# The in-projection of a short convolution by seven half-size products instead of eight, and weights laid out in order of use

## The chip, the cores and the metric

One NeuronCore of a Trainium2 chip runs the whole program in one launch. The metric is the device time of one execution in microseconds. Times of the kernel before: three runs, median 1492.78 us (1491.48 to 1495.35). TensorE (PE) does the matrix products, VectorE (DVE) and ScalarE (ACT) the elementwise work, GpSimd (POOL) a little, and SyncE (SP) issues the loads. A matmul multiplies a stationary block of 128x128 weights with up to 512 columns of tokens and adds into PSUM.

## The reference

Four layers, each with its own token mixer (HGRN2, short convolution, RG-LRU, latent attention), over 512 latent and 128 prompt tokens, T = 640 in all, at width 1024:

```
x <- LayerNorm(alpha * x + gate * Mixer(x * (1 + scale) + shift))
```

Scale, shift and gate come from a conditioning vector times a 1024x3072 matrix per layer (`ada_w`). The change is in layer 1, whose mixer is, for the modulated input h:

```
bg, cg, v, g = split(h @ w_in, 4)          # w_in is 1024 x 4096
y = depthwise_conv(cg * v, width 3) + b
out = (bg * y * silu(g)) @ w_out
```

## The kernel before, in words

All products are float32 by three products of a rounded form: each operand is kept as a high part (`xh`, `wh`) and a low part (`xl`, `wl`), and hi x hi, hi x lo and lo x hi are added in PSUM. Tokens lie along the free dimension, as 8 blocks (KT = 8) of 128 channels by 640 tokens.

Weights come in blocks of 128 x 1024 numbers (512 KB). `_prep` (L57) loads one into a raw tile (L71, for a column block of 128 outputs in runs of 128 numbers, 512 B), has ScalarE cast the high part (L74) and VectorE subtract it for the low part (L76, at high priority). Raw tiles have 3 buffers (NR, tag `wraw`), high and low tiles 4 (NW). `next_w` (L94) keeps three blocks ready ahead, and before that pumps the ada units: each call adds a rate (0.4 in this stage) to a credit, and a whole credit runs one `ada_unit` (L205), two loads of 512 KB into the same raw tiles and 8 matmuls (L230) of the conditioning of a later layer, summed by VectorE at L232.

`sconv` (L806) runs over j = 0..7, and for each takes four output tiles of 128 channels, in the order cg, v, bg, g. A tile is made by `mtile` (L120): 8 blocks x 3 products x 2 token halves = 48 matmuls of 320 columns (L136) into two PSUM banks. ScalarE copies cg (L821), VectorE multiplies it with v straight from PSUM (L823), ScalarE makes the middle tap (L828), VectorE the two outer ones in four pieces (L803), multiplies by bg (L840), and applies silu(g) (ScalarE tanh at L386, L388) into `o` (L843), the input of the out-projection (`pso`, L116 to L118). For j = 0 the first pair, and for j = 7 the last, run by `mpair` (L140), which takes two tiles together in token pieces of 384 and 256, since the next or the last tokens come late. Between, `affine` (L292, L293) finishes tokens of the layer before.

PSUM has two buffers of two banks for these tiles (`psmm`) and four of one bank for all else (`psg`). A list scheduler with priorities sets the order of the instructions of each engine; each engine then runs its own in that order, and waits on tiles as a whole: an instruction that overwrites a tile waits for its readers.

Of the kernel before, what the change touches and what calls it, by code (L numbers as in the profile page):

```python
# [16 lines left out]
P = 128  # L17
# [28 lines left out]

class Kernel:
# [4 lines left out]
    def weights(self, items):  # L52
        self.wq = list(items)
        self.wready = []
        self.wpos = 0

    def _prep(self):  # L57
        nc = self.nc
        parts = self.wq[self.wpos]
        if isinstance(parts, tuple):  # L60
            parts = [parts]
        i = self.wpos
        self.wpos += 1
        n = sum(a * b for _, (a, b) in parts)
# [12 lines left out]
        self.wready.append(res)  # L77
# [42 lines left out]
    def mtile(self, nk=KT, xh=None, xl=None, halves=False):  # L120
# [17 lines left out]
        return out  # L138

# [65 lines left out]
    def ada_unit(self, l, c, u):  # L205
# [15 lines left out]
        for k in (2 * u, 2 * u + 1):  # L221
            raw = self.rawp.tile([P, 1024], F32, name=f"araw{l}_{c}_{k}", tag="wraw")
            w = self.I["ada_w"][l][k * P:(k + 1) * P, :]
            if c == 2:
                nc.sync.dma_start(out=raw, in_=w[:, 2 * D:3 * D])
            else:
                nc.sync.dma_start(out=raw.rearrange("p (a n) -> p a n", a=2),
                                  in_=w.rearrange("p (a n) -> p a n", a=3)[:, 0:2, c * 512:(c + 1) * 512])
# [115 lines left out]
    def norm_tile(self, l, i, s, stats, tp, last):  # L344
# [19 lines left out]
        def rest():  # L364
            for j0 in range(0, KT, 4):
                h = tp.tile([P, 4, P], F32, name="hm", tag="hm")
# [34 lines left out]
    def start(self):  # L401

        nc, tc = self.nc, self.tc
        with ExitStack() as ctx:
# [29 lines left out]
            def part(q, u):  # L434

                raw = tp.tile([P, 2, 2, 256], F32, name=f"araw0_{q}_{u}", tag="araw", bufs=NA)
                for k in range(2):
                    w = self.I["ada_w"][0][(2 * u + k) * P:(2 * u + k + 1) * P, :].rearrange("p (a n) -> p a n", a=3)
                    nc.sync.dma_start(out=raw[:, k], in_=w[:, 0:2, q * 256:(q + 1) * 256])
# [36 lines left out]

    def hgrn_weights(self):
        w = self.I["hg_w_in"]
        it = []

        def col(c0):
            return (w[:, c0:c0 + P].rearrange("(k p) n -> p k n", p=P), (KT, P))
        for kind, h in self.HG_ORDER:
            if kind == "g":
                it.append(col(4096 + h * P))
                continue
            it.append(col(1024 + h * P))
            it.append(col(2048 + h * P))
            it.append(col(h * P))
            if h % 2 == 0:  # L490
                for kk in range(2):
                    it.append((w[kk * 512:(kk + 1) * 512, 3072 + h * P:3072 + (h + 2) * P]
                               .rearrange("(k p) n -> p k n", p=P), (4, 256)))
        return it + self.out_weights(self.I["hg_w_out"])

    @staticmethod
    def out_weights(w):
        it = []
        for c0 in (0, 256):
            for kk in range(2):  # L500
                it.append((w[kk * 512:(kk + 1) * 512, c0:c0 + 256].rearrange("(k p) n -> p k n", p=P), (4, 256)))
        for kk in range(4):
            it.append((w[kk * 256:(kk + 1) * 256, 512:1024].rearrange("(k p) n -> p k n", p=P), (2, 512)))
        return it
# [283 lines left out]
    def sconv_weights(self):  # L788
        w = self.I["sc_w_in"]
        it = []  # L790
        for j in range(KT):
            for g in (1, 2, 0, 3):
                c0 = g * D + j * P
                it.append((w[:, c0:c0 + P].rearrange("(k p) n -> p k n", p=P), (KT, P)))
        return it + self.out_weights(self.I["sc_w_out"])

# [9 lines left out]
    def sconv(self):  # L806
        nc, tc = self.nc, self.tc
        with ExitStack() as ctx:
            sp = ctx.enter_context(tc.tile_pool(name="sp", bufs=1))
            for j in range(KT):  # L810
                cg = sp.tile([P, T], F32, name="cg", tag="cg")
                p = sp.tile([P, T], F32, name="pcv", tag="pcv")
                if j == 0:
                    pss = self.mpair()
                    for hf in range(2):
                        c = SPL[hf]
                        nc.scalar.copy(out=cg[:, c], in_=pss[hf][:, 0])
                        nc.vector.tensor_tensor(out=p[:, c], in0=cg[:, c], in1=pss[hf][:, 1], op=ALU.mult)
                else:
# [10 lines left out]
                bz = sp.tile([P, T], F32, name="bz", tag="bz")  # L830
                if j == KT - 1:
                    pss = self.mpair()
                    for hf in range(2):
                        c = SPL[hf]
                        nc.vector.tensor_tensor(out=bz[:, c], in0=zz[:, c], in1=pss[hf][:, 0], op=ALU.mult)
                        sg = self.silu2h(sp, pss[hf][:, 1], ("silut", "sg")[hf])
                        nc.vector.scalar_tensor_tensor(out=self.o[:, j, c], in0=sg, scalar=0.5, in1=bz[:, c], op0=ALU.mult, op1=ALU.mult)
                    break
                ps = self.mtile()
                nc.vector.tensor_tensor(out=self.hv(bz), in0=self.hv(zz), in1=ps, op=ALU.mult)  # L840
                ps = self.mtile()
                sg = self.silu2(sp, ps, "sg")
                nc.vector.scalar_tensor_tensor(out=self.o[:, j, :], in0=sg, scalar=0.5, in1=bz, op0=ALU.mult,  # L843
                                               op1=ALU.mult)
                if 1 <= j <= NT:
                    self.affine(0, j - 1)

# [3 lines left out]

    def rg_weights(self):
        w, wg = self.I["rg_w_in"], self.I["rg_w_gate"]
        it = []
        for kind, r in self.RG_ORDER:
            if kind == "b":
                for d in range(2):
                    it.append((wg[d, r].rearrange("(k p) n -> p k n", p=P), (2, 512)))
            else:
                for a in range(2):  # L860
                    c0 = (D if kind == "g" else 0) + (2 * r + a) * P
                    it.append((w[:, c0:c0 + P].rearrange("(k p) n -> p k n", p=P), (KT, P)))
        return it + self.out_weights(self.I["rg_w_out"])
# [152 lines left out]

    def mla_weights(self):
        w, wq, wkv = self.I["mla_w_in"], self.I["mla_w_qb"], self.I["mla_w_kvb"]

        def blk(m, r0, nr, c0, nco):  # L1020
            return (m[r0 * P:(r0 + nr) * P, c0:c0 + nco].rearrange("(k p) n -> p k n", p=P), (nr, nco))
        gt = [blk(w, 0, KT, 672 + j * P, P) for j in range(KT)]
        it = gt[:2] + [blk(w, 2 * i, 2, 0, 384) for i in range(4)]
        it += [blk(w, 3 * i, min(3, KT - 3 * i), 384, 288) for i in range(3)] + gt[2:]
        it += [blk(wq, 0, 2, 1024, 512), blk(wq, 2, 1, 1024, 512)]
        for g in range(4):
            it.append(blk(wkv, 0, 2, 1024 + g * 256, 256))
            for p in range(2):
                c = (2 * g + p) * P
                it.append([blk(wkv, 0, 2, c, P), blk(wq, 0, 3, c, P)])  # L1030
        return it + self.out_weights(self.I["mla_w_out"])
# [388 lines left out]
    def build(self):  # L1420
# [50 lines left out]

def _consts():
# [57 lines left out]
```

## Time and profile before

| | |
|---|---|
| median of three runs | 1492.78 us |
| the profiled execution | 1496.1 us, span 1494.2 us |
| TensorE, matmuls | 1443.9 us busy, 97% of the span, 10738 records |
| VectorE | 998.2 us, 67% |
| ScalarE | 695.6 us, 47% |
| GpSimd | 91.8 us, 6% |
| chain that ended last, by engine | PE 72%, DVE 13%, ACT 8%, DMA 3% |
| L136 of that chain | 26% |
| loads by the SP queue | 153.58 MB, 32.8% of 16 engines' span |

A busy time is the union of an engine's records. A chain is followed back from the last instruction, at each step to what released it. Matmuls overlap in their records: what one costs is the distance from start to start. The short-convolution stage lies between about 516 and 800 us, its in-projection between 516 and 757.9.

### The profile page before, as it was taken

What the parts mean: (1) busy time and instruction counts of PE and PEld (TensorE: products, weight loads), DVE (VectorE), ACT (ScalarE), POOL (GpSimd) and SP (SyncE); (2) the same over time, 40 slices, a digit from 0 to 9 for tenths busy, and PEclk for the clock granted to TensorE, in tenths of its full rate; (3) what the DMA queues carried; (4) which work ended last, traced back from release to release, by engine and by line L of the source; (5) the groups of instructions that cost most, each with busy time, mean ns of one, the idle gap of its engine ahead of it and who ended that gap; (6) DMA issues with size and microseconds to landing.
All of it is one profiled execution on the core that took longest, in us unless ns stands there. A gap on an engine that the chain in (4) does not pass through costs nothing.

```text
span 1494.2 us, 26291 instructions
## 1 busy us (share of the span) xinstructions
PE 1443.9 (97%) x10738; PEld 1322.2 (88%) x10738; DVE 998.2 (67%) x1833; ACT 695.6 (47%) x1213; POOL 91.8 (6%) x194
## 2 busy tenths in 40 slices
PE   6999999999999999999999999999999999999997
PEld 4888989989989899999997889899899988888796
DVE  4677677477576734444376799787746778677767
ACT  2556456356353522122225477733642366666630
POOL 0000000000000100000001011120110200000002
PEclk8999999999999999999999999999999999999999
DMA  9422334224326144435431344443123200001031
GB/s 322 134 65 78 93 101 147 91 67 140 103 63 239 57 130 124 141 114 156 128 113 57 113 156 145 129 152 123 53 81 99 82 19 17 25 21 37 29 141 71
DMA packets 159192, 155.25 MB, mean 104 GB/s; under 512 B 6288, under 2 KB 130272, under 8 KB 159072
## 3 DMA queue, kind: packets, MB, share of 16 engines
q1 hardware_dynamic: 159072, 153.58, 32.8%
q8 instruction: 84, 1.38, 0.4%
q14 instruction: 36, 0.29, 0.1%
HBM read 147.07 MB, written 6.48 MB: 103 GB/s over the span
## 4 chain that ended last, share of the span: by engine, by line
PE 72%; DVE 13%; ACT 8%; DMA 3%; issue 3%; POOL 1%; SPq 1%; POOLq 0%; DVEq 0%; ACTq 0%
PE psmm L136 26%; PE pso L116 4%; PE pso L118 4%; PE pso L117 4%; PE poa L1345 3%; DVE wl L76 2%; PE ptp L1332 2%; PE psmm L117 2%; PE psmm L118 2%; PE psmm L960 2%; PE psmm L116 2%; PE psA L230 2%; PE psS L116 1%; PE psS L118 1%; PE psS L117 1%
## 5 line engine op out<-in xcount | busy, mean ns | idle before, releaser
L136 PE MATMUL psmm<-xh,wh 128*128 128x320 f32 x1200 | 283.8, 316 | 2.5 <-ACT vt L604 2.1
L136 PE MATMUL psmm<-xl,wh 128*128 128x320 f32 x1200 | 277.9, 312 | 0.0
L136 PE MATMUL psmm<-xh,wl 128*128 128x320 f32 x1200 | 276.3, 311 | 0.0
L74 ACT CAST wh<-wraw 128x1024 fp32r<-128x1024 f32 (+3 forms) x157 | 156.4, 1005 | 150.9 <-PE pso L118 55.6
L76 DVE TENSOR_TENSOR wl<-wraw,wh 128x1024 fp32r<-128x1024 f32 (+3 forms) x157 | 182.3, 1170 | 57.2 <-ACT wh L74 57.0
L136 PEld LDWEIGHTS psmm<-xh,wh 128*128 128x128 f32 x1200 | 200.6, 189 | 15.9 <-issue 7.5
L136 PEld LDWEIGHTS psmm<-xl,wh 128*128 128x128 f32 x1200 | 201.6, 189 | 3.7 <-issue 3.4
L136 PEld LDWEIGHTS psmm<-xh,wl 128*128 128x128 f32 x1200 | 201.9, 189 | 0.7 <-issue 0.5
L116 PE MATMUL pso<-wh,xh 128*128 128x256 f32 (+1 forms) x464 | 149.7, 323 | 0.0
L117 PE MATMUL pso<-wl,xh 128*128 128x256 f32 (+1 forms) x464 | 148.6, 320 | 0.0
L118 PE MATMUL pso<-wh,xl 128*128 128x256 f32 (+1 forms) x464 | 148.6, 320 | 0.0
L118 PEld LDWEIGHTS pso<-wh,xl 128*128 128x128 f32 x464 | 87.3, 188 | 7.3
L116 PEld LDWEIGHTS pso<-wh,xh 128*128 128x128 f32 x464 | 87.4, 188 | 7.1 <-ACT xh L104 0.4
L117 PEld LDWEIGHTS pso<-wl,xh 128*128 128x128 f32 x464 | 87.4, 188 | 6.6
L1316 ACT ACTIVATE pe<-psS,mx 128x768 f32<-128x768 f32 (+1 forms) x80 | 63.7, 797 | 38.9 <-DVE mx L1314 38.4
L1314 DVE TENSOR_REDUCE mx<-psS 128x1 f32<-128x768 f32 (+1 forms) x80 | 65.3, 817 | 7.8 <-PE psS L118 7.1
L373 ACT ACTIVATE hm<-pt,ab 128x128 f32<-128x128 f32 x108 | 41.1, 463 | 50.0 <-PE pt L369 50.0
L117 PE MATMUL psmm<-xl,wh 128*128 128x384 f32 (+1 forms) x192 | 59.8, 311 | 1.6 <-DVE xl L107 1.6
L118 PE MATMUL psmm<-xh,wl 128*128 128x384 f32 (+1 forms) x192 | 59.2, 308 | 1.1 <-DVE wl L76 1.1
L116 PE MATMUL psmm<-xh,wh 128*128 128x384 f32 (+1 forms) x192 | 59.7, 311 | 0.0
L1332 PE MATMUL ptp<-ident,pe 128*128 128x128 f32 x400 | 56.7, 273 | 0.8 <-ACT pe L1316 0.8
L326 DVE TENSOR_TENSOR t<-pso,gateb 128x256 f32<-128x256 f32 (+1 forms) x58 | 29.4, 511 | 37.1 <-PE pso L118 35.9
(424 smaller groups left out, 3013.7 us busy)
## 6 DMA issues: line engine op xcount, KB each, us to landing
araw<-in_ada_w SPq DMA_DIRECT2D x80, 512.0 KB
wraw<-in_hg_w_in SPq DMA_DIRECT2D x40, 512.0 KB
wraw<-in_sc_w_in SPq DMA_DIRECT2D x32, 512.0 KB
araw<-in_ada_w SPq DMA_DIRECT2D x32, 256.0 KB
wraw<-in_rg_w_in SPq DMA_DIRECT2D x16, 512.0 KB
wraw<-in_hg_w_out SPq DMA_DIRECT2D x8, 512.0 KB
gateb<-gate_dram SPq DMA_DIRECT2D x8, 512.0 KB
wraw<-in_sc_w_out SPq DMA_DIRECT2D x8, 512.0 KB
```

Source lines behind the costliest of these rows:

```text
L74: self.tc.keep_in_program_order(nc.scalar.copy(out=wh[:, :n], in_=raw[:, :n]))
L76: nc.vector.tensor_tensor(out=wl[:, :n], in0=raw[:, :n], in1=wh[:, :n].bitcast(F32), op=ALU.subtract)
L116: nc.tensor.matmul(ps, lhsT=ah, rhs=bh, start=(i == 0), stop=False)
L117: nc.tensor.matmul(ps, lhsT=ah, rhs=bl, start=False, stop=False)
L118: nc.tensor.matmul(ps, lhsT=al, rhs=bh, start=False, stop=(i == n - 1))
L136: nc.tensor.matmul(ps[hf][:, :HALF], lhsT=w[:, k, :], rhs=x[:, k, hf * HALF:(hf + 1) * HALF], start=(first and k == 0), stop=(last and k = ...
L230: nc.tensor.matmul(ps[32 * j:32 * j + 32, :], lhsT=self.csil[:, k, :], rhs=raw[:, j * 256:(j + 1) * 256], start=(k == 2 * u), stop=(k == 2 ...
L373: nc.scalar.activation(out=h[:, j, :], in_=pt[:, j, :], func=AF.Identity, scale=sc, bias=bi)
L1314: nc.vector.reduce_max(out=mx, in_=ps[:, :nk], axis=AX.X, negate=True)
L1316: nc.scalar.activation(out=pe[:, :nk], in_=ps[:, :nk], func=AF.Exp, bias=mx[:, 0:1], accum_out=g["sm"][:, n, hp:hp + 1])
L1332: nc.tensor.transpose(pt[:, kk, :], pe[:, (k0 + kk) * P:(k0 + kk + 1) * P], self.ident)
L1345: nc.tensor.matmul(po[hp * 64:(hp + 1) * 64, 0, :nq], lhsT=v4[:, kt, vc + hp * 64:vc + (hp + 1) * 64], rhs=g["pt"][hp][:, kk, :nq], start= ...
```

## The change

Four things are done.

**Pairs by seven products.** Two output tiles of a pair and the two token halves make a 2x2 block product, with the 8 channel blocks in two groups of 4. `spair` computes it by Strassen's scheme with seven products a, b, s2, s1, s3, s4, d, each 4 blocks x 3 = 12 matmuls of 320 columns: 84 in place of 96. Product a runs into one half of a PSUM tile (`psxz`), is copied out (L224) and kept, and s2 and s3 go on in the same half, with a copy behind each; s1 and s4 use the other half, b a bank of its own (`psy`); d ends the first half. VectorE and ScalarE form the outputs (L234, L241, L242, L245). All pairs of the stage run so but the first of j = 0.

**Weight sums.** `_prep_pair` loads a pair's two blocks, A|B and D|C, casts and splits A|B (tile `w`), and D (tile `wd`, one buffer), adds in place in the raw tiles (L111: D' = C - or + D and so on, four adds of 512), and casts and splits the sums into `ws` (s1, s3; two buffers) and another `w` tile (s2, s4). `next_w` prepares a pair where 4 blocks have room.

**Token sums.** `token_sums` forms three sums of the token blocks from h, which layer 0's norm now leaves in `self.o`, by four VectorE operations of 4 x 320, and splits four.

**Layout.** The host packs all weight blocks into `wpack` in order of use, so that each partition's row of a block is one run of 4 KB; `ada_first` and `ada_rest` do the same for the conditioning matrix. The first ada loads are 16 of 512 KB, before 32 of 256 KB.

The core of the diff:

```diff
     def _prep(self):
...
-        for src, (a, b) in parts:
-            nc.sync.dma_start(out=raw[:, o:o + a * b].rearrange("p (a b) -> p a b", a=a), in_=src)
+        w0 = P * self.woff[i]
+        nc.sync.dma_start(out=raw[:, :n], in_=self.I["wpack"][w0:w0 + P * n].rearrange("(p n) -> p n", p=P))
+        for _, _, a, _, b in parts:
...
+    def _prep_pair(self):
...
+        (a, b), (d, c) = ((r[:, 0:512], r[:, 512:1024]) for r in raws)
+
+        def halves(pool, nm, n):
+            return [pool.tile([P, n], F32R, name=f"{nm}{s}{i}", tag=f"{nm}{s}", bufs=1 if n == 512 else None)
+                    for s in "hl"]
+
+        def cast(o, r):
+            for k in range(0, r.shape[-1], 512):
+                nc.scalar.copy(out=o[0][:, k:k + 512], in_=r[:, k:k + 512])
+
+        def low(o, r):
+            nc.vector.tensor_tensor(out=o[1], in0=r, in1=o[0].bitcast(F32), op=ALU.subtract)
+
+        def add(o, x, y):
+            nc.vector.tensor_tensor(out=o, in0=x, in1=y, op=ALU.add)
+        wab, wd, s13, s24 = (halves(self.wp, "w", 1024), halves(self.sw, "wd", 512), halves(self.sw, "ws", 1024),
+                             halves(self.wp, "w", 1024))
+        with self.tc.high_priority():
+            cast(wab, raws[0])
+            cast(wd, d)
+            low(wab, raws[0])
+            low(wd, d)
+            add(d, c, d)
+            add(c, a, c)
+            cast(s13, raws[1])
+            add(a, d, a)
+            add(b, a, b)
+            cast(s24, raws[0])
+            low(s13, raws[1])
+            low(s24, raws[0])
...
     def next_w(self):
-        self.pump(self.rate)
-        la = NW - 1
-        while len(self.wready) < la and self.wpos < len(self.wq):
-            self._prep()
-        return self.wready.pop(0)
+        self.pump(self.rate * (2 if self.wready and self.wready[0][0] == 2 else 1))
+        while self.wpos < len(self.wq):
+            have = sum(n for n, _ in self.wready)
+            if isinstance(self.wq[self.wpos], Pair):
+                if self.sw is None or have + 2 > NW:
+                    break
+                self._prep_pair()
...
+    def spair(self, pool, n):
...
+        prod(x, "a", [v[:, lo, N1] for v in (self.xh, self.xl)], True)
+        p1 = keep(x, "p1")
+        prod(y, "b", [v[:, hi, N1] for v in (self.xh, self.xl)], True)
+        prod(x, "s2", t[2], False)
+        u2 = keep(x, "u2")
+        with self.tc.high_priority():
+            nc.vector.tensor_tensor(out=oa[:, N1], in0=p1, in1=y, op=ALU.add)
+        prod(z, "s1", t[1], True)
+        p5 = keep(z, "p5")
+        prod(x, "s3", t[3], False)
+        u3 = keep(x, "u3", "p1")
+        prod(z, "s4", [v[:, hi, N2] for v in (self.xh, self.xl)], False)
+        with self.tc.high_priority():
+            nc.vector.scalar_tensor_tensor(out=ob[:, N2], in0=u3, scalar=-1.0, in1=p5, op0=ALU.mult, op1=ALU.subtract)
+            nc.vector.tensor_tensor(out=oa[:, N2], in0=u2, in1=z, op=ALU.add)
+        prod(x, "d", t[4], False)
+        with self.tc.high_priority():
+            nc.scalar.mul(out=ob[:, N1], in_=x, mul=-1.0)
+        return oa, ob
...
     def sconv(self):
...
+            self.sw = ctx.enter_context(tc.tile_pool(name="sw", bufs=2))
...
-                    ps = self.mtile()
-                    nc.scalar.copy(out=self.hv(cg), in_=ps)
-                    ps = self.mtile()
-                    nc.vector.tensor_tensor(out=self.hv(p), in0=self.hv(cg), in1=ps, op=ALU.mult)
+                    p, v = self.spair(sp, 0)
+                    nc.vector.tensor_tensor(out=p, in0=p, in1=v, op=ALU.mult)
...
+                bg, g = self.spair(sp, 1)
```

Line numbers of the changed kernel that the orders below show: L95 the load of a pair's raw tile, L105 the casts, L108 the low parts, L111 the adds, L218 the matmuls, L224 the copies, L234, L241, L242 and L245 the outputs, L890 the taps, L911 cg times v, L916 the middle tap, L921 to L925 bg, silu and `o`. `wdh60` is the high part of the d block of the pair of weight blocks 60 and 61, `wdl60` its low part, `wsh60` and `wsl60` its sums s1 and s3; `wh60` and `wl60` stand for its A|B, and under the later numbers 6488 and 6489 for its sums s2 and s4; `t2h`, `t2l` and so on are the token sums.

**TensorE, in the middle of the stage, between two tiles, before.** `wh58` and `wh59` are the weight blocks of two tiles:

```order
L136 MATMUL psmm_6415<-xh_102,wh58_6270 128x320 x2
L136 MATMUL psmm_6415<-xl_103,wh58_6270 128x320 x2
L136 MATMUL psmm_6415<-xh_102,wl58_6271 128x320 x2
L136 MATMUL psmm_6471<-xh_102,wh59_6340 128x320 x2
L136 MATMUL psmm_6471<-xl_103,wh59_6340 128x320 x2
```

**TensorE, at the third product of the pair 60, now.** Ahead of these rows stand the 12 matmuls of product d of the pair 58 and nine of product b of the pair 60:

```order
L218 MATMUL psy_6654<-xl_103,wh60_6482 128x320
L218 MATMUL psy_6654<-xh_102,wl60_6483 128x320
L218 MATMUL psxz_6653<-t2h_5851,wh60_6488 128x320
L218 MATMUL psxz_6653<-t2l_5852,wh60_6488 128x320
L218 MATMUL psxz_6801<-xh_102,wh62_6630 128x320
L218 MATMUL psxz_6801<-xl_103,wh62_6630 128x320
L218 MATMUL psxz_6653<-t2h_5851,wl60_6489 128x320
```

Where a tile's matmuls followed those of the tile before, s2 now follows b, with two matmuls of product a of the pair 62 between its own first ones.

**ScalarE at the same place, before**, with `sgt` the tanh of g, `cg` the copy and `zz` the middle tap:

```order
L74 CAST wh58_6270<-wraw58_6269 128x1024
L821 COPY cg_6267<-psmm_6275 128x640
L74 CAST wh59_6340<-wraw59_6339 128x1024
L828 ACTIVATE zz_6395<-pcv_6268,vec_72 128x640
L74 CAST wh60_6410<-wraw60_6409 128x1024
L74 CAST wh61_6466<-wraw61_6465 128x1024
L386 ACTIVATE sgt_6520<-psmm_6471 128x640
L74 CAST wh62_6544<-wraw62_6543 128x1024
```

**ScalarE, now.** `psxz_6505` belongs to the pair 58, `psxz_6653` to the pair 60:

```order
L224 COPY u3_6576<-psxz_6505 128x320
L224 COPY p1_6669<-psxz_6653 128x320
L105 CAST wdh60_6484<-wraw61_6480 128x512
L245 ACTIVATE cb1_6508<-psxz_6505 128x320
L922 ACTIVATE th_6605<-cb1_6508 128x640
L105 CAST wsh60_6486<-wraw61_6480 128x512 x2
L105 CAST wh60_6488<-wraw60_6478 128x512
L105 CAST wh62_6630<-wraw62_6626 128x512 x2
L105 CAST wh60_6488<-wraw60_6478 128x512
L224 COPY u2_6695<-psxz_6653 128x320
```

The cast of a block depended on its load and on a free tile three blocks back; now the cast of `wdh60` stands behind the copies of the pair 58 and writes the one `wd` tile, which product d of the pair 58 reads.

**VectorE at the same place, before**, with `pcv` the product cg times v:

```order
L76 TENSOR_TENSOR wl58_6271<-wraw58_6269,wh58_6270 128x1024
L292 TENSOR_TENSOR z_5047<-z_5047,lng0_6261 128x1024
L293 TENSOR_TENSOR z_5047<-z_5047,lnb0_6263 128x1024
L232 TENSOR_TENSOR arows2_5864<-psA2_0_3_6325,arows2_5864 128x256
L76 TENSOR_TENSOR wl59_6341<-wraw59_6339,wh59_6340 128x1024
L823 TENSOR_TENSOR pcv_6268<-cg_6267,psmm_6345 128x640
L254 SCALAR_TENSOR_TENSOR mods2_85<-psT2_0_6402,vec_72 128x4 x4
```

**VectorE, now**, the same pair 60:

```order
L108 TENSOR_TENSOR wdl60_6485<-wraw61_6480,wdh60_6484 128x512
L111 TENSOR_TENSOR wraw61_6480<-wraw61_6480 128x512
L234 TENSOR_TENSOR ca0_6655<-p1_6669,psy_6654 128x320
L111 TENSOR_TENSOR wraw61_6480<-wraw60_6478,wraw61_6480 128x512
L923 SCALAR_TENSOR_TENSOR cb1_6508<-th_6605,cb1_6508 128x640
L111 TENSOR_TENSOR wraw60_6478<-wraw61_6480,wraw60_6478 128x512
L108 TENSOR_TENSOR wsl60_6487<-wraw61_6480,wsh60_6486 128x1024
L111 TENSOR_TENSOR wraw60_6478<-wraw60_6478 128x512
L925 SCALAR_TENSOR_TENSOR o_104<-cb1_6508,ca1_6507 128x640
L108 TENSOR_TENSOR wl60_6489<-wraw60_6478,wh60_6488 128x1024
```

Between two low parts there stood the elementwise work of one tile; now the low part of d, four in-place adds and two more low parts stand in one run, with L234, L923 and L925 between them.

## Rows read from the trace of the kernel before

**Rows 1.** Page, section 1: busy time, share of the span, instructions of each engine.
```profile
PE 1443.9 (97%) x10738; PEld 1322.2 (88%) x10738; DVE 998.2 (67%) x1833; ACT 695.6 (47%) x1213; POOL 91.8 (6%) x194
```

**Rows 2.** Windows: span, busy PE, PEld, DVE, ACT, POOL, clock, DMA share, GB/s.
```profile
550.00:575.00 25.00, 25.00 (x180) 24.22 (x180) 8.71 (x12) 4.55 (x5) 0.00 (x0) 1.00 0.46 141
```

**Rows 3.** Chain of waits, sconv stage: start, duration, engine, tile, line, count.
```profile
533.04 14.29 PE psmm L136 x96
547.33 1.00 PE psA L230 x16
...
757.93 0.12 PE pso L116
```

**Rows 4.** Timeline of PE, 552 to 580: start, duration, instruction, count.
```profile
554.82 0.46 PE L136 MATMUL psmm<-xl,wh 128*128 128x320 f32 x2
555.11 0.46 PE L136 MATMUL psmm<-xh,wl 128*128 128x320 f32 x2
```

**Rows 5.** Groups by line and form, 520 to 750: busy, mean ns, idle before.
```profile
L76 DVE TENSOR_TENSOR wl<-wraw,wh 128x1024 fp32r<-128x1024 f32 x32 | 38.8, 1221 | 24.9 <-ACT wh L74 24.9
L803 DVE SCALAR_TENSOR_TENSOR zz<-pcv,vec,zz 128x511 f32<-128x511 f32 x16 | 12.0, 748 | 6.2 <-ACT zz L828 6.2
L843 DVE SCALAR_TENSOR_TENSOR o<-sg,bz 128x640 f32<-128x640 f32 x7 | 5.8, 822 | 0.1
L803 DVE SCALAR_TENSOR_TENSOR zz<-pcv,vec,zz 128x127 f32<-128x127 f32 x16 | 5.5, 345 | 0.0
L107 DVE TENSOR_TENSOR xl<-hm,xh 128x512 fp32r<-128x512 f32 x3 | 2.0, 691 | 0.1
L104 ACT CAST xh<-hm 128x512 fp32r<-128x512 f32 x3 | 1.9, 620 | 0.1
L817 ACT COPY cg<-psmm 128x384 f32<-128x384 f32 x1 | 0.5, 472 | 0.0
```

**Rows 6.** Timeline of DVE, 572 to 590.
```profile
580.33 1.22 DVE L76 TENSOR_TENSOR wl<-wraw,wh 128x1024 fp32r<-128x1024 f32 x1
581.46 1.22 DVE L292 TENSOR_TENSOR z<-z,lng 128x1024 f32<-128x1024 f32 x1
582.72 1.23 DVE L293 TENSOR_TENSOR z<-z,lnb 128x1024 f32<-128x1024 f32 x1
```

**Rows 7.** Timeline of ACT, 553 to 580.
```profile
555.66 0.69 ACT L821 COPY cg<-psmm 128x640 f32<-128x640 f32 x1 [6.66 <-PE psmm L136]
...
571.40 1.05 ACT L74 CAST wh<-wraw 128x1024 fp32r<-128x1024 f32 x1 [5.99 <-DMA wraw<-in_sc_w_in]
```

**Rows 8.** Timeline of SP, the queue that issues the loads, 560 to 575.
```profile
567.36 3.29 SPq L71 DMA_DIRECT2D wraw<-in_sc_w_in  x2
```

**Rows 9.** Timeline of PE around an idle stretch in HGRN2.
```profile
314.75 0.66 PE L680 MATMUL pst<-ident,ku 128*128 128x128 f32 x4 [2.07 <-DVE ku L675]
...
315.86 0.73 PE L136 MATMUL psmm<-xh,wl 128*128 128x320 f32 x2
316.39 0.73 PE L136 MATMUL psmm<-xh,wh 128*128 128x320 f32 x2
```

**Rows 10.** Windows of 1 us behind that idle stretch.
```profile
315.00:316.00 1.00, 1.00 (x8) 1.00 (x7) 0.95 (x3) 1.00 (x3) 0.00 (x0) 0.73 0.00 0
...
318.00:319.00 1.00, 1.00 (x7) 1.00 (x7) 1.00 (x4) 0.28 (x1) 0.00 (x0) 0.57 0.00 0
```

**Rows 11.** Chain of waits at the start of the program.
```profile
16.87 7.18 DMA araw<-in_ada_w
24.09 1.29 PE psQ L443 x16
```

**Rows 12.** Windows of 2 us: loads in 1-KB runs, loads in 4-KB runs.
```profile
28.00:30.00 2.00, 2.00 (x22) 0.98 (x21) 0.00 (x0) 0.00 (x0) 0.00 (x0) 0.82 1.09 384
...
1436.00:1438.00 2.00, 2.00 (x19) 2.00 (x18) 0.68 (x3) 0.00 (x0) 0.00 (x0) 1.00 1.02 410
```

More of the change, by code (lines that the diff above doesn't have):

```diff
@@ L44 @@
 NVEC = _o
+class Pair(list):
+    pass
 class Kernel:
@@ L53, in weights @@
         self.wq = list(items)
+        self.woff = [0]
+        for parts in self.wq:
+            self.woff.append(self.woff[-1] + sum(a * b for _, _, a, _, b in parts))
         self.wready = []
@@ L59, in _prep @@
         parts = self.wq[self.wpos]
-        if isinstance(parts, tuple):
-            parts = [parts]
         i = self.wpos
         self.wpos += 1
-        n = sum(a * b for _, (a, b) in parts)
+        n = sum(a * b for _, _, a, _, b in parts)
         raw = self.rawp.tile([P, 1024], F32, name=f"wraw{i}", tag="wraw")
@@ L76, in _prep, with part @@
             nc.vector.tensor_tensor(out=wl[:, :n], in0=raw[:, :n], in1=wh[:, :n].bitcast(F32), op=ALU.subtract)
-        self.wready.append(res)
+        self.wready.append((1, res))
+    def _prep_pair(self):
+        nc = self.nc
+        i = self.wpos
+        self.wpos += 2
+        raws = []
+        for n in range(2):
+            raw = self.rawp.tile([P, 1024], F32, name=f"wraw{i + n}", tag="wraw")
+            w0 = P * self.woff[i + n]
+            nc.sync.dma_start(out=raw, in_=self.I["wpack"][w0:w0 + P * 1024].rearrange("(p n) -> p n", p=P))
+            raws.append(raw)
+        (a, b), (d, c) = ((r[:, 0:512], r[:, 512:1024]) for r in raws)
[24 more added lines that the diff above has]
+            low(s24, raws[0])
+        def part(o, k):
+            return [x[:, 512 * k:512 * k + 512].rearrange("p (a b) -> p a b", a=4) for x in o]
+        self.wready.append((2, dict(a=part(wab, 0), b=part(wab, 1), d=part(wd, 0), s1=part(s13, 0), s3=part(s13, 1),
+                                    s2=part(s24, 0), s4=part(s24, 1))))
     def pump(self, rate):
@@ L138, in mtile, with prod, keep @@
         return out
+    def spair(self, pool, n):
+        nc = self.nc
+        w = self.next_w()
+        N1, N2 = slice(HALF, T), slice(0, HALF)
+        lo, hi = slice(0, 4), slice(4, KT)
+        t = self.tops
+        xz = self.psmm.tile([P, 2, 512], F32, name="psxz", tag="mm")
+        y = self.psg.tile([P, 512], F32, name="psy", tag="g")
+        x, z, y = xz[:, 0, :HALF], xz[:, 1, :HALF], y[:, :HALF]
+        def prod(ps, wk, b, first):
+            (ah, al), (bh, bl) = w[wk], b
+            for k in range(4):
+                for u, v, st, en in ((ah, bh, True, False), (ah, bl, False, False), (al, bh, False, True)):
+                    nc.tensor.matmul(ps, lhsT=u[:, k, :], rhs=v[:, k, :], start=(first and st and k == 0),
+                                     stop=(en and k == 3), skip_group_check=True)
+        def keep(ps, nm, tag=None):
+            o = pool.tile([P, HALF], F32, name=nm, tag=tag or nm)
+            with self.tc.high_priority():
+                nc.scalar.copy(out=o, in_=ps)
+            return o
+        oa = pool.tile([P, T], F32, name=f"ca{n}", tag=f"ca{n}")
+        ob = pool.tile([P, T], F32, name=f"cb{n}", tag="cb")
+        prod(x, "a", [v[:, lo, N1] for v in (self.xh, self.xl)], True)
[14 more added lines that the diff above has]
+        prod(x, "d", t[4], False)
+        with self.tc.high_priority():
+            nc.scalar.mul(out=ob[:, N1], in_=x, mul=-1.0)
+        return oa, ob
@@ new lines, in token_sums, with parts @@
+    def token_sums(self, pool):
+        nc, o = self.nc, self.o
+        N1, N2 = slice(HALF, T), slice(0, HALF)
+        lo, hi = slice(0, 4), slice(4, KT)
+        b11, b12, b21, b22 = o[:, lo, N1], o[:, lo, N2], o[:, hi, N1], o[:, hi, N2]
+        def parts(n):
+            return [pool.tile([P, 4, HALF], F32R, name=f"t{n}{s}", tag=f"t{n}{s}") for s in "hl"]
+        t = {1: [v[:, lo, N2] for v in (self.xh, self.xl)], 2: parts(2), 3: parts(3), 4: parts(4)}
+        nc.vector.tensor_tensor(out=b11, in0=b11, in1=b12, op=ALU.subtract)
+        nc.vector.tensor_tensor(out=b12, in0=b22, in1=b12, op=ALU.subtract)
+        nc.vector.scalar_tensor_tensor(out=b22, in0=b22, scalar=-1.0, in1=b11, op0=ALU.mult, op1=ALU.subtract)
+        self.split(*t[2], b22)
+        self.split(*t[1], b11)
+        self.split(*t[3], b12)
+        nc.vector.scalar_tensor_tensor(out=b21, in0=b22, scalar=-1.0, in1=b21, op0=ALU.mult, op1=ALU.subtract)
+        self.split(*t[4], b21)
+        self.tops = t
@@ L222, in ada_unit @@
             raw = self.rawp.tile([P, 1024], F32, name=f"araw{l}_{c}_{k}", tag="wraw")
[L223 to L228, printed above, removed]
+            nc.sync.dma_start(out=raw, in_=self.I["ada_rest"][l, c, k])
             for j in range(4):
@@ L436, in part @@
                 raw = tp.tile([P, 2, 2, 256], F32, name=f"araw0_{q}_{u}", tag="araw", bufs=NA)
-                for k in range(2):
-                    w = self.I["ada_w"][0][(2 * u + k) * P:(2 * u + k + 1) * P, :].rearrange("p (a n) -> p a n", a=3)
-                    nc.sync.dma_start(out=raw[:, k], in_=w[:, 0:2, q * 256:(q + 1) * 256])
+                nc.sync.dma_start(out=raw.rearrange("p k a n -> p (k a n)"), in_=self.I["ada_first"][4 * q + u])
                 ps = acc[q % 2][:, q - q % 2, :]
@@ L829, in sconv @@
                 self.taps(zz, p, (-1, 1), (cw(0), cw(2)))
[L830 to L838, printed above, removed]
```

175 lines of the change are left out of this document (91 added, 84 removed).

## The prediction

> **What bounds the kernel now.** I read the page's busy times first: TensorE is busy for 97% of the span, VectorE for 67%, ScalarE for 47% [rows 1]. An average over eleven stages does not say what this stage hides, so I read windows of 25 us over the short-convolution stage next: TensorE is busy in every microsecond at the full granted clock, VectorE for 8.7 of 25 us [rows 2]. Then the chain of waits: it runs on TensorE alone, 96 matmuls of the in-projection in 14.29 us, two ada units of 8 matmuls each in 1.00 us, and the next stage's first matmul at 757.93 [rows 3]. The pitch of two 320-column matmuls in the timeline is 0.29 us, so 0.147 us each [rows 4]; the 0.46 us beside it is the modelled record of two overlapping ones, not their price. So before, every matmul that goes is time, provided that its operands are ready. What I have to find out is whether they are.
>
> **What the change takes from TensorE.** Fifteen pairs lose 12 of 96 matmuls: 15 x 12 x 0.147 = 26.5 us. A pair took 14.29 us, and 14.7 with its ada share: 0.4 units for each of its two blocks, a unit being 8 matmuls or 0.5 us [rows 3]. It would take 84 x 0.147 + 0.4 = 12.7 us. This is the gain if nothing waits.
>
> **What it adds: a chain that can't start early.** `wd` has one buffer. The orders show what follows: ScalarE's cast of the next pair's d block can't be made until product d of the pair before has read the old one, and product d is a pair's last. Behind that cast stand, each on the one before: the low part of d, the add that overwrites d in the raw tile, the add into c, the add into a, the add into b, the cast of that sum, its low part, and only then s2, the third product. Call the end of product d zero and count a link at a time. Durations: 1.22 us for a low part of 1024, 0.82 for 640, 0.75 for a tap of 511, 0.35 for one of 127, 0.69 for 512, 0.62 for ScalarE's cast of 512, 0.47 for its copy of 384 out of PSUM [rows 5]. An instruction that needn't wait for the one ahead starts 0.08 us before that one's record ends (580.33 to 581.46 is 1.13 for a 1.22), one that needs it 0.03 behind (1.26 for a 1.22) [rows 6]; from engine to engine I take 0.1 us (the last matmul ends at 555.57, ScalarE's copy starts at 555.66 [rows 4, 7]). A 320-element VectorE operation is not in the trace; from the 512 and 640 forms it is about 0.49.
> - Behind a pair whose outputs are bg and g: cast 0.72, low of d 0.73, add 0.72, L234 0.40, add 0.61, L923 0.74, add 0.61, low of s1/s3 1.14, add 0.61, L925 0.74, low of s2/s4 1.14: 8.2 us.
> - Behind a pair whose outputs are cg and v: cast 0.72, low 0.73, L911 0.74, L234 0.40, three adds 1.83, the four tap pieces 0.67 + 0.27 + 0.67 + 0.27, low 1.14, add 0.61, low 1.14: 9.2 us.
>
> Without the fill-ins between the links (L234, L890, L911, L923, L925 and the low of s1/s3) it is six dependent steps and 6.2 us, so no order on these engines hides it.
>
> TensorE meanwhile has 11 matmuls of product b, 2 of s2 and 2 of the a after next: 2.2 us. From the last low part it issues 69 matmuls to the end of the next d (10 + 4 + 12 + 1 + 12 + 4 + 12 + 2 + 12): 10.1 us, with 0.5 for ada. Each of s1, s3, s4 and d also waits for a copy or an add that empties the PSUM half it goes on with: 0.2 to the record's end, 0.1, about 0.42 for 320 elements (below the 0.47 of 384 [rows 5]), 0.1, in all 0.8 us, against fill-ins of 4 matmuls, of ada, of 4 matmuls and of ada: some 1.1 us are left over the four. That is 11.7 us. **A cycle is 11.7 + 8.7 = 20.4 us**, in place of 14.7 at most.
>
> **The clock.** Behind an idle stretch of 2.07 us the granted clock fell to half: the pitch of two matmuls went to 0.53 us [rows 9], and by the share in the windows (0.73 in the first, 0.57 in the last [rows 10]) it stayed at 1.2 GHz for about 3.4 us. At the start of the program it stayed there for 4.6 us behind the first psQ at 24.09, until the window with 0.82 [rows 11, 12]. Here TensorE idles for 8.7 - 2.2 = 6.5 us in each cycle, so I expect each to pay: half of 3.4 to 4.6 us is 1.7 to 2.3. Slower fill-ins give back up to half a microsecond, as they cover more of the copies. I take 1.3 (0 to 2.3): **21.7 us a cycle**.
>
> **Ends of the stage.** The first in-projection pair stays. For pair 0, VectorE has `token_sums` besides: four operations and four low parts of 1280 elements, from the 640 and 1024 forms [rows 5] some 1.5 us each, 12 in all, and 6.4 us of weight work, from about 526 on; a and b of pair 0 and those of pair 1, pulled ahead, are 7 us of cover. Before, pair 0 ended at 547.33. I take 553 for its d (548 to 557). Then 14 cycles: 553 + 14 x 21.7 = 856.8, against 757.9: +98.9 us. The last pair's elementwise work, in halves, now stands between d and the last output matmuls: +1 (0 to 2). `next_w` pumps the ada units at the same rate per block, so they cost what they did.
>
> **The layout.** Where loads already lie behind TensorE, longer runs are worth nothing, and that is nearly everywhere. At the start they don't: TensorE's first psQ waits 7.18 us for `araw` [rows 11]. Loads in 1-KB runs went at 384 GB/s, loads in 4-KB runs at 410 [rows 12]; 6% of the 20 us to 24.09 is -1.3 us (0 to -3). The Trainium skill ("DMA: Bandwidth & Descriptors", Specifications) puts the smallest transfer that runs at line rate at 512 B; by that the start gains nothing and the sum is 1.3 us higher. The rows say that 1-KB runs aren't at the rate of 4-KB runs, and I go by them. In the stage, a load that is issued at 567.36 is cast at 571.40, 4.0 us later [rows 7, 8]; three raw buffers now serve two pairs and two ada loads, and the first ada load of a cycle, which waits for the last low part, comes about when TensorE wants it: 0 to +0.6 a cycle, taken as 0, since slower cycles leave more room.
>
> **Sum.** +98.9 + 1 - 1.3 = +98.6 on the profiled execution of 1496.1 us, so 1594.7. The median of the runs, 1492.78, lies 3.3 below that execution: **1591 us**.
>
> **Rivals.**
> - *The buffer does not bind, the engines overlap as before* (faster). If the cast of d needn't wait, the preparation runs a pair ahead; VectorE's work per two pairs, about 23 us by the same durations, fits beside 25.4 of TensorE. Then -26.5 - 1.3 + 2 for pair 0: 1467 us. The windows, with VectorE at a third [rows 2], speak for it; the order, in which each cast stands behind the copies of the pair before, against. It decides where the chain from the end of d falls under 14.5 - 11.7 = 2.8 us. 0.06.
> - *The chain binds, the clock holds or the links are shorter.* At 20.4 a cycle it is 18 us less: 1573; with a microsecond less of fill-ins as well, 1559. One idle stretch in HGRN2 [rows 9] is not a steady round of them. 0.15.
> - *The clock is at half for all of TensorE's part of a cycle*: 14 x (10.6 - 1.3) = 130 more, 1721. Nothing in rows 9 to 12 shows half speed with the engine fed for longer than 4.6 us. 0.03.
> - *The change doesn't do what it says*: the blocks come in time because the scheduler's order leaves TensorE other work, and only matmuls and fill-ins trade places, 1492 give or take 4. The order shows 15 matmuls of cover and no more. 0.01.
>
> My forecast has 0.75. Its own range: cycles at 2.3 for the clock (+14), loads late by 0.6 (+8) and pair 0 at 557 (+4) give 1617; the lower end goes into the second rival. The range that I give runs from 1555 to 1618. A measurement here tells 0.3%, 4.5 us, from no change: faster 0.06, same 0.01, slower 0.93.
>
> **What would show it.** Right: TensorE idles 5 to 7 us in each pair just ahead of s2, released by VectorE's low part at L108, and that one goes back over L111 and the casts at L105 to product d; the in-projection takes about 340 us; the granted clock dips in every window of 25 us there; the first psQ comes 1 to 2 us earlier. Wrong: TensorE is busy for 95% of the stage or more, or the idle time ends on a load, on a PSUM copy, or on `token_sums`. If the cycle is about 20 us and the clock stays at 1.00, only the clock's term was wrong; if it is over 23 with idle stretches of 8 us, a link of the chain is dearer than its row.

## The result, and the profile after

The changed kernel takes 1606.73 us, median of four runs (1605.22 to 1607.83), against 1492.86 in four runs before: a ratio of 1.076, 95% interval 1.0741 to 1.0779. It is 114 us slower; 98 slower was forecast, and the range, 1555 to 1618, holds the time. The profiled execution has a span of 1605.2 us, 111.0 more than before.

The page of the changed kernel: busy times, and the granted clock over 40 slices.

```profile
PE 1467.5 (91%) x10558; PEld 1327.5 (83%) x10558; DVE 1091.3 (68%) x1976; ACT 759.2 (47%) x1360; POOL 91.6 (6%) x194
...
PEclk9999999999999988788889999999999999999999
```

TensorE, at 97% before [rows 1], is at 91%, and its clock is below 0.9 in seven slices of the stage. TensorE's longest waits between 510 and 900 us: what waited, for what, total, times, longest.

```profile
PE psxz L218 <- ACT wh L105: 59.7, 14, 6.4
PE psxz L218 <- DVE wl L108: 23.0, 14, 2.2
PE pt L496 <- DVE z L485: 2.3, 1, 2.3
PE psxz L218 <- ACT u L224: 1.5, 3, 0.6
```

Fourteen times, once a pair from the second on, TensorE waits ahead of s2 up to 6.4 us for the casts of the sums at L105, issues a few matmuls, and waits again, up to 2.2 us, for their low part: 82.7 us, 5.9 a pair. No copy out of PSUM and no load has more than 1.5 us. In windows of 25 us, with the columns of [rows 2]:

```profile
600.00:625.00 25.00, 17.15 (x85) 15.57 (x84) 14.59 (x24) 7.39 (x14) 0.00 (x0) 0.77 0.20 59
...
675.00:700.00 25.00, 20.06 (x123) 17.32 (x123) 12.99 (x17) 7.34 (x14) 0.00 (x0) 0.84 0.27 84
```

From 550 to 875 TensorE is busy for 16 to 20 of 25 us, where it was busy for all of them. VectorE has 11 to 15, so it isn't VectorE's total work that TensorE waits for, but the order of that work. The chain of waits through one gap: start, duration, what.

```profile
637.03 1.62 PE psxz L218 x11
...
638.68 0.63 ACT wdh L105
...
639.33 0.70 DVE wdl L108
...
640.06 0.69 DVE wraw L111
640.75 0.40 DVE ca L234
641.15 0.60 DVE wraw L111
641.75 0.74 DVE cb L923
642.48 0.60 DVE wraw L111
643.08 1.14 DVE wsl L108
644.22 0.60 DVE wraw L111
644.82 0.73 DVE o L925
645.56 1.18 DVE wl L108
...
646.78 3.30 PE psxz L218 x11
```

Product d of one pair ends at 638.65; ScalarE's cast of the next d block starts at 638.68; then low part, add, L234, add, L923, add, low part, add, L925 and the last low part follow without a hole, and s2 goes on at 646.78. From the end of d that is 8.1 us; the forecast had 8.2 for this kind of pair. For the other kind the same view has 616.17 to 625.12, 9.0 us, against 9.2.

The cycle is read from ScalarE's L245, which empties d's bank: the first of the stage and the last one, fourteen pairs apart.

```profile
549.22 0.43 ACT L245 ACTIVATE cb<-psxz 128x320 f32<-128x320 f32 x1
...
867.43 0.44 ACT L245 ACTIVATE cb<-psxz 128x320 f32<-128x320 f32 x1
```

318.2 / 14 = 22.7 us a pair, where 21.7 was forecast and two tiles took 14.29 before [rows 3].

The clock through one gap, windows of 1 us (length, PE, PEld, DVE, ACT, POOL, clock, DMA share, GB/s):

```profile
616.00:617.00 1.00, 0.75 (x6) 0.48 (x4) 0.15 (x1) 0.81 (x2) 0.00 (x0) 1.00 0.00 0
...
621.00:622.00 1.00, 0.03 (x1) 0.03 (x1) 1.00 (x2) 0.69 (x2) 0.00 (x0) 0.76 0.00 0
...
628.00:629.00 1.00, 1.00 (x7) 0.95 (x7) 0.00 (x0) 0.43 (x1) 0.00 (x0) 0.83 0.03 12
```

TensorE stopped at 616.8; the clock fell to half in 621 to 622, and came back in 628 to 629, 3 us behind the last low part. In the cycle before this one it was at half until 607.9, 6.1 us behind it.

Against the stage, the start of the program has become shorter, and by more than was forecast. TensorE's first psQ behind loads comes at 22.73, before at 24.09 [rows 11]:

```profile
22.73 1.08 PE L568 MATMUL psQ<-araw,csil 128*32 128x128 f32 x16 [3.21 <-DMA araw<-in_ada_first]
```

and by the last psQ, the end of the first layer's conditioning, the lead is 6.5 us. The chain of before:

```profile
29.73 0.36 PE psQ L443 x8
30.09 0.63 PE psmm L136 x3
30.72 0.35 PE psQ L443 x8
31.07 0.79 PE psmm L136 x4
31.86 0.35 PE psQ L443 x8
...
50.98 0.11 PE psQ L451
```

and of the changed kernel:

```profile
37.90 0.57 PE psQ L568 x16
38.48 1.22 PE psmm L198 x7
39.70 0.57 PE psQ L568 x16
...
44.51 0.11 PE psQ L576
```

In this stretch TensorE changes between the conditioning (`psQ`) and matmuls of the first layer (`psmm`). Before, a load of 256 KB gave a piece of 8 records; now one of 512 KB gives 16. The same 16 records and 7 matmuls take 31.86 - 29.73 = 2.13 us before and 39.70 - 37.90 = 1.80 us now, both at full clock. Behind the first psQ, TensorE's list of waits has no wait for a load in this stretch, in either kernel.

The first matmul of the stage and the first of the next layer's stage, in the timeline of TensorE before:

```profile
516.19 0.42 PE L116 MATMUL psmm<-xh,wh 128*128 128x384 f32 x1
...
853.38 0.46 PE L960 MATMUL psmm<-uh,wh 128*128 128x320 f32 x2
```

and after:

```profile
508.08 0.42 PE L178 MATMUL psmm<-xh,wh 128*128 128x384 f32 x1
...
964.92 0.46 PE L1030 MATMUL psmm<-uh,wh 128*128 128x320 f32 x2
```

So the stage begins 8.1 us earlier and the next one 111.5 us later: the pairs cost 119.6 us, and the layout gives 8.1 back.

### The profile page after: what moved, and what is told of

It is laid out like the page before. It is cut to its first block, busy times and chain, and to the rows that moved or that the text cites. A ratio compares the mean times of both kernels' runs of the same rounds, so it can differ in the third digit from the quotient of the medians.

```text
span 1605.2 us, 26178 instructions
## 1 busy us (share of the span) xinstructions
PE 1467.5 (91%) x10558; PEld 1327.5 (83%) x10558; DVE 1091.3 (68%) x1976; ACT 759.2 (47%) x1360; POOL 91.6 (6%) x194
## 4 chain that ended last, share of the span: by engine, by line
PE 67%; DVE 19%; ACT 8%; issue 3%; DMA 2%; POOL 1%; SPq 0%; POOLq 0%; DVEq 0%; ACTq 0%
PE psmm L198 13%; PE psxz L218 11%; PE pso L179 4%; PE pso L180 4%; PE pso L178 4%; PE poa L1399 3%; DVE wraw L111 2%; PE psmm L1030 2%; DVE wl L82 2%; PE psA L354 2%; PE ptp L1386 2%; PE psmm L179 1%; PE psS L178 1%; PE psS L180 1%; PE psmm L180 1%
## 5 line engine op out<-in xcount | busy, mean ns | idle before, releaser
L198 PE MATMUL psmm<-xh,wh 128*128 128x320 f32 x752 | 179.5, 317 | 2.2 <-ACT vt L700 1.7
L80 ACT CAST wh<-wraw 128x1024 fp32r<-128x1024 f32 (+5 forms) x127 | 125.2, 996 | 118.7 <-PE pso L180 62.7
L198 PE MATMUL psmm<-xh,wl 128*128 128x320 f32 x752 | 174.8, 312 | 0.0
L198 PE MATMUL psmm<-xl,wh 128*128 128x320 f32 x752 | 174.1, 312 | 0.0
L82 DVE TENSOR_TENSOR wl<-wraw,wh 128x1024 fp32r<-128x1024 f32 (+5 forms) x127 | 145.8, 1158 | 29.8 <-ACT wh L80 29.5
L198 PEld LDWEIGHTS psmm<-xh,wh 128*128 128x128 f32 x752 | 126.1, 189 | 9.8 <-issue 3.5
L198 PEld LDWEIGHTS psmm<-xl,wh 128*128 128x128 f32 x752 | 126.3, 189 | 2.6 <-issue 2.0
L198 PEld LDWEIGHTS psmm<-xh,wl 128*128 128x128 f32 x752 | 126.9, 189 | 0.9 <-issue 0.8
L218 PE MATMUL psxz<-t2h,wh 128*128 128x320 f32 x60 | 29.0, 484 | 59.7 <-ACT wh L105 59.7
L241 DVE SCALAR_TENSOR_TENSOR cb<-u,p 128x320 f32<-128x320 f32 x15 | 7.4, 493 | 106.4 <-ACT u L224 106.4
L218 PEld LDWEIGHTS psxz<-t2h,wh 128*128 128x128 f32 x60 | 18.3, 305 | 63.7 <-ACT wh L105 63.3
L224 ACT COPY u<-psxz 128x320 f32<-128x320 f32 x30 | 12.8, 427 | 96.6 <-PE psxz L218 96.6
```

What stands on the lines that cost most here:

```text
L80: self.tc.keep_in_program_order(nc.scalar.copy(out=wh[:, :n], in_=raw[:, :n]))
L82: nc.vector.tensor_tensor(out=wl[:, :n], in0=raw[:, :n], in1=wh[:, :n].bitcast(F32), op=ALU.subtract)
L198: nc.tensor.matmul(ps[hf][:, :HALF], lhsT=w[:, k, :], rhs=x[:, k, hf * HALF:(hf + 1) * HALF], start=(first and k == 0), stop=(last and k = ...
L218: nc.tensor.matmul(ps, lhsT=u[:, k, :], rhs=v[:, k, :], start=(first and st and k == 0), stop=(en and k == 3), skip_group_check=True)
```

## The experiments

Ratios are to the kernel before, in runs on the same chip (medians there 1494.0 and 1494.4). Differences to the changed kernel are between runs on different chips.

### Two buffers for the d block

```diff
-            return [pool.tile([P, n], F32R, name=f"{nm}{s}{i}", tag=f"{nm}{s}", bufs=1 if n == 512 else None)
+            return [pool.tile([P, n], F32R, name=f"{nm}{s}{i}", tag=f"{nm}{s}", bufs=None)
...
-                th = sp.tile([P, T], F32, name="th", tag="th")
+                th = zz
```

> The d block gets two buffers instead of one; to make room the tanh of g is written over the dead middle-tap tile. Theory (the one buffer starts the chain of weight sums only at the end of product d): the chain runs a pair ahead, TensorE no longer idles ahead of s2, the granted clock stays at 1.00 in the stage, a cycle falls from 22.8 to about 13.3 us, and the time from 1606.7 to about 1475 (1465 to 1490). Rival (VectorE's work or the loads of the pair are the bound, whatever the buffer): the cycle stays at 20 us or more, 1565 to 1610.

Measured: 1479.92 us, ratio 0.9897 (0.9878 to 0.9917). Two buffers take 127 us off the changed kernel, and what results takes 1% less than the kernel before. A window of the stage:

```profile
575.00:600.00 25.00, 25.00 (x173) 23.03 (x172) 21.77 (x36) 12.26 (x24) 0.00 (x0) 1.00 0.37 109
```

From 550 to 725 the clock is at 1.00; TensorE is busy for 25.0 us in five of the seven windows and for 23.2 and 24.1 in the others, with VectorE at 19 to 22 of 25 us beside it. What TensorE still waits for in the products of the pairs, and for the layer norm ahead of them:

```profile
PE psxz L218 <- DVE ca L242: 2.4, 2, 1.8
PE pt L496 <- DVE z L485: 2.4, 1, 2.4
...
PE psxz L218 <- ACT u L224: 1.8, 3, 1.1
...
PE psxz L218 <- ACT p L224: 1.4, 2, 0.8
```

The casts and low parts of the pairs' weights are gone from the list. L245, first and last:

```profile
548.58 0.43 ACT L245 ACTIVATE cb<-psxz 128x320 f32<-128x320 f32 x1
...
743.29 0.44 ACT L245 ACTIVATE cb<-psxz 128x320 f32<-128x320 f32 x1 [1.03 <-PE psxz L218]
```

194.7 / 14 = 13.9 us a pair. The theory is borne out; it had 13.3. The rival, VectorE's total or the loads as the bound at 20 us, is out.

### The tanh moved, one buffer

The control for the line that made room: only `th = zz`.

> The changed kernel with one buffer for the d block, and the tanh of g written over the dead middle-tap tile as in the run with two buffers. Theory (the second buffer alone made the difference there): no change from the changed kernel, 1603 to 1611. Rival (moving the tanh behind the product with bg took a step out of the chain): 1590 or less.

Measured: 1608.91 us, ratio 1.0769 (1.0752 to 1.0786); the changed kernel had 1.076 (1.0741 to 1.0779). Moving the tanh alone changes nothing; the second buffer makes the difference.

### Product d ahead of s4

```diff
+        prod(x, "d", t[4], False)
...
         prod(z, "s4", [v[:, hi, N2] for v in (self.xh, self.xl)], False)
...
-        prod(x, "d", t[4], False)
```

> In each pair product d is issued ahead of s4 instead of behind it, with one buffer for the d block as in the changed kernel; the work is the same. Theory (the chain starts at the end of product d): s4 moves into the time of the chain, the idle time ahead of s2 falls by some 1.8 us a pair and the cycle with it: 14 x 1.8 = 25 us less, about 1582 (1570 to 1590). Rival (the wait ahead of s2 ends on a load or on VectorE's total work): 1604 to 1610.

Measured: 1565.06 us, ratio 1.0478 (1.0459 to 1.0497), 42 us less than the changed kernel. The same work, the same one buffer, another order of two products. TensorE's waits:

```profile
PE psxz L218 <- DVE wl L108: 26.4, 14, 2.5
PE psxz L218 <- ACT wh L105: 18.5, 14, 2.3
```

44.9 / 14 = 3.2 us a pair, 2.7 less. Not only the 12 matmuls of s4 (1.8 us) now run beside the chain, but one of the two pieces of ada too (8 records, 0.57 us), which the scheduler puts behind d, and three matmuls of the next products. A cycle, from one emptying of d's bank (L242 in this run) to the next, is 19.4 us, 3.4 less; the 0.7 beyond the idle time was not taken apart. The time lies below the range expected. That the wait hangs on the place of d is shown by this a second time. The chain is no longer the same everywhere, though: in two of the three cycles between 600 and 645 us it runs from the end of s4 over the sum that VectorE takes from its bank (L245, at 623.93 in one of them), and not straight from d.

### Matmuls in the gap

```diff
         prod(y, "b", [v[:, hi, N1] for v in (self.xh, self.xl)], True)
+        for _ in range(30):
+            nc.tensor.matmul(z, lhsT=w["b"][0][:, 0, :], rhs=self.xh[:, 0, N1], start=True, stop=True, skip_group_check=True)
         prod(x, "s2", t[2], False)
```

> The changed kernel with 30 more matmuls of 320 columns for each pair between products b and s2, into the half bank that s1 then overwrites; their results are not used. They need about 4.4 us at full clock and nothing of the chain. Theory (the idle time is set by the chain, and 2.4 us of each cycle are the lower clock that the idle time brings): the clock stays near 1.00 in the stage, the cycle falls to about 20.4 us and the time to about 1573 (1565 to 1585), with 450 matmuls more. Rival (the clock costs nothing, the phase behind s2 is slow for another reason): no change, 1604 to 1610. Rival (TensorE is the bound): 15 x 4.4 = 66 us more, 1673.

Measured: 1596.30 us, ratio 1.068 (1.066 to 1.07): 450 matmuls more and 10 us less. The first rival (no effect) and the second (66 us more) are both out, but the gain is a third of what was expected. A window of the stage:

```profile
575.00:600.00 25.00, 22.07 (x149) 19.54 (x148) 15.27 (x22) 9.22 (x17) 0.00 (x0) 1.00 0.34 106
```

The clock is at 1.00 for most of the stage, and the cycles there are 20.0 to 21.1 us behind one kind of pair and 21.1 to 21.9 behind the other. In three of the first thirteen, with waits of 1.9 to 2.1 us ahead, the clock still fell to half, and they took 22.7 to 24.1; behind waits of 2.06 us at 579, 620 and 794 it stayed at 1.00. The thirteen have a mean of 21.35. The phase behind the last low part can be read here at full clock:

```profile
640.51 4.27 PE psxz L218 x26
644.78 0.57 PE psA L356 x8
645.35 4.64 PE psxz L218 x29
649.99 0.57 PE psA L356 x8
...
651.05 1.62 PE psxz L218 x11
```

12.2 us to the end of d; with chains of 8.1 and 9.0 a cycle is 20.7. So the clock costs the changed kernel 22.7 - 20.7 = 2.0 us a cycle. The last pair ate part of the gain; it has no next pair to fill its copies' waits with:

```profile
840.00:842.00 2.00, 1.48 (x6) 1.08 (x5) 0.00 (x0) 0.42 (x1) 0.00 (x0) 0.50 0.01 4
```

In each window of 2 us that holds a change of product TensorE is idle for some half a microsecond, and the clock stays at 0.50 from 838 to 852. The products take 3.58 us for 12 matmuls there, and this one cycle 26.7 us; in the changed kernel the last cycle is 21.8.

### The layout alone

The kernel before, with `wpack`, `ada_first` and `ada_rest`, and `sconv`, `weight_list` and the layer norm's output as they were:

> The kernel before with the packed layout of all weights and nothing else of the change: the stage is computed by 48 matmuls a tile as before. By the prediction's term for the start (6% of the first 20 us): 1491.5, that is 1.3 us less than before. By the trace of the changed kernel, which reaches the stage's first matmul at 508.1 where before had 516.4: 8 us less, about 1484.5. Rival (the earlier arrival is taken back at the first wait for a layer norm): 1490 to 1493.

Measured: 1486.24 us, ratio 0.9944 (0.9924 to 0.9964), 7.8 us less than the runs of before on that chip. The stage's first matmul in the timeline:

```profile
504.99 0.42 PE L178 MATMUL psmm<-xh,wh 128*128 128x384 f32 x1
```

11.2 us ahead of before in this profiled execution, whose own time (1482.65) is 3.6 under the median of its runs. The forecast's 1.3 us, as the worth of the whole layout, falls; the lead read from the changed kernel holds, and no later wait takes it back.

### Without the token sums

Of the kernel with two buffers, `token_sums` is left out, and the products take token blocks of the input:

```diff
-        t = {1: [v[:, lo, N2] for v in (self.xh, self.xl)], 2: parts(2), 3: parts(3), 4: parts(4)}
...
+        t = {n: [v[:, lo, N2] for v in (self.xh, self.xl)] for n in (1, 2, 3, 4)}
```

> The kernel with two buffers for the d block, without the token sums: their four VectorE operations and four splits are left out and the products take plain token blocks in their place, so the stage's numbers are other ones; the rest of the work is the same. Theory (of the 26.5 us of matmuls saved, a good part is lost at the start of the stage, where VectorE is busy for 24.6 of 25 us with the token sums and the weights of two pairs): 12 us of VectorE work less there give 6 to 9 us, 1472 to 1474. Rival (the start is set by the layer norm of the last tokens and by TensorE, the sums are covered): 1478 to 1481, no change.

Measured: 1482.34 us, ratio 0.9917 (0.9899 to 0.9936): no gain over 0.9897 (0.9878 to 0.9917). The theory misses. L245 of pair 0 comes at 544.98, 3.6 us ahead of the kernel with two buffers, but the pair after next at 574.29, against 574.06. No waiting lies between: from 520 to 575, TensorE has no wait over 0.5 us in either run. It had issued 12 matmuls of pair 1 by the end of d of pair 0, and 29 with the sums; 17 matmuls are 2.5 of the 3.6 us. Mostly the order is another one, and the sums were covered.

### The preparation of pair 0 behind the first pair

```diff
-            self.sw = ctx.enter_context(tc.tile_pool(name="sw", bufs=2))
+            sw = ctx.enter_context(tc.tile_pool(name="sw", bufs=2))
...
                     pss = self.mpair()
+                    self.sw = sw
```

> The kernel with two buffers for the d block, and the weights of pair 0 prepared only behind the first in-projection pair instead of ahead of it. Theory (its preparation, at high priority, holds back the layer norm of the last tokens, and TensorE waits 2.4 us for it): the wait for z goes, 2 us less, about 1478. Rival (the weights of pair 0 then come late and cost more than the wait): 2 to 8 us more, 1482 to 1488.

Measured: 1490.27 us, ratio 0.9975 (0.9966 to 0.9984), 10 us more than with the early preparation. TensorE's longest waits:

```profile
PE psxz L218 <- issue: 5.9, 1, 5.9
PE psxz L218 <- DVE wl L108: 2.2, 1, 2.2
```

The wait for z is gone, and in its place stand 5.9 us for which the profile shows no releaser, and 2.2 for a low part. The rival holds, with a larger price than its 2 to 8 us: the 2.4 us that the early preparation costs buy more than they take.

## Why the prediction was right, and where its sizes were off

**The mechanism** was the one that is now shown: one buffer of `wd`, the cast behind product d, a chain of dependent links, TensorE idle ahead of s2. The second buffer removes it, the other order shortens it, and the control leaves it. The links, taken from rows of the kernel before, sum to 8.2 and 9.2; they measure 8.1 and 9.0. (The "six dependent steps" are eight in the prediction's own list; nothing rests on the count.)

**The phase**, from the last low part to the end of the next d, was 11.7 and measures 12.2 at full clock. The term that was too small is ada: "8 matmuls or 0.5 us a unit". The 16 records in 1.00 us [rows 3] are one unit, not two: the trace has two records for each of these matmuls (192 between 520 and 750 us, beside 12 of the sums at L232, one a unit). Most pairs thus carry 16 records, 1.14 us with the switches between, in place of 0.5.

**The clock's term**, taken as 1.3 within 0 to 2.3, measures 2.0. It was read from a stretch that fell to half behind 2 us of idle time and was back 3.4 us later [rows 9, 10]. Here the clock fell inside the gap, and came back 3 to 6 us behind the last low part. Base and clock together: 20.7 + 2.0 = 22.7, 1.0 above the forecast, times 14: 14.4 us.

**Pair 0** was put at 553 (548 to 557). It ends at 548.7, with a stage that begins 8.1 earlier: 556.8 on the scale of the prediction, 3.8 late, at the end of its bounds. 2.3 us are the wait for the layer norm of the last tokens (z, L485), which the early preparation of pair 0 holds back on VectorE. Behind it the clock was at half for 3.4 us (0.56, 0.50, 0.50 and 0.73 in the windows of 1 us from 519), which is 1.7 us more. Neither was in the sum.

**The tail** was +1 and is +2: from d's end to the next layer's first matmul 97.5 us, where the end of the last tile before left 95.5.

**The layout** was -1.3 (0 to -3) and is -8.1 in the trace, 7.8 in the run alone. To the first psQ behind loads the term held: 24.09 - 22.73 = 1.4. The step that failed is "Where loads already lie behind TensorE, longer runs are worth nothing", by which all behind that psQ was put at nothing. From there to the last psQ it is 26.9 us before and 21.8 after, 5.1 less, and TensorE does not wait for a load there: its records touch each other, and its list of waits has none. The 192 records of psQ come in 23 pieces before and in 12 after. At 2.13 - 1.80 = 0.33 us, 11 pieces fewer are 3.6 us; and 10 matmuls of the first layer fewer lie in the stretch (69 for 79), 1.5 us. So most of it is the size of a load, which sets how often TensorE changes between two products, and not the rate of the loads. This is read from the traces; a run with the longer runs and the old size of a load was not made. The last 1.6 of the 8.1 us were not taken apart. By the rule of the Trainium skill ("DMA: Bandwidth & Descriptors", Specifications), full rate from 512 B on, longer runs would have had no gain at all. The windows of [rows 12] have 384 and 410 GB/s, and the 1.4 us to the first psQ are about what that difference gives, so the measurement decides against using it here.

In all: +98.9 for the stage became +117.6, +1 became +2.0, -1.3 became -8.1; +98.6 became +111.5, which is the span's +111.0 within the reading. The in-projection took 359 us, where about 340 was named. That the sum is 12.9 us off and not 19.7 is luck: the layout gave back 6.8 us that its term did not have, for a reason that the prediction did not see.

**The rivals.** The first one, at 0.06, named what would have had to be so: a cast that needn't wait for d. With the second buffer it came out at 1479.9, where 1467 was worked out. Of the 1.76 us a pair that twelve matmuls cost, 15.0 - 13.9 = 1.1 seems to arrive (15.0 being two tiles with their ada, 210.4 us from 547.33 to 757.77 over 14). Some 0.4 of the rest goes to the waits of the list above (5.6 us over 14 pairs, without the one for z). Fourteen pairs thus bring 15.7 us from d to d, but what the seven-product scheme leaves over the layout alone is 1486.2 - 1479.9 = 6.3. The traces show where the rest goes. From the stage's first matmul to the next layer's it is 332.9 us with two buffers (508.65 to 841.52) and 337.2 before, 4.3 less. The tail is 2.6 us longer, and L245 of pair 0 comes 39.9 us behind the stage's first matmul, where pair 0 took 31.1 before: 8.8 more. In these 8.8 lie the wait for z (2.4), 3.4 us at half clock behind it (1.7), and the 29 matmuls of pair 1 that are issued ahead of the end of this d (4.3). The last are work of the fourteen pairs that the count from d to d leaves out; put back, they leave 0.8 us a pair of the 1.76, not 1.1. Smaller terms of either sign were not taken apart, and the token sums are not it.

## What to carry to other kernels

Before counting what a scheme saves on the bound engine, follow one tile of each pool from its last reader to its next writer: a single buffer whose reader is the last instruction of a step makes everything behind the writer serial, and here 4 KB more a partition were worth 127 us, where the matmuls saved were worth 26.5 at most. Count that chain link by link from rows of the kernel at hand; this held within 3%. Price a small piece of work by how often the engine has to change to it and back, too: half as many pieces were worth some 3.6 us at the start. If there is no room for the buffer, issue its reader earlier: moving twelve matmuls past it was worth 42 us.

## What the runs showed of the hardware that I had not expected

Once TensorE's clock had fallen, short pauses went with a clock that stayed low. In the last pair of the run with matmuls in the gap, it had fallen behind the usual gap, and with pauses of about half a microsecond at each change of product it then stayed at 1.2 GHz for 14 us, the engine being busy for 1.4 to 2.0 of every 2 us. In the middle of that stage it mostly stayed at 2.4 GHz over one pause a cycle of 1.7 us on average. And filling a gap with matmuls whose results nobody uses made the kernel 10 us faster.
